# Feed-forward entry of a two-layer encoder: transposes behind the per-layer projection, products grouped by part

## The chip, the cores and the metric

The kernel runs on one core of a Trainium2 chip. The metric is device time in microseconds, the median of several runs. Before the change it is 927.31 us over three runs (926.59 to 927.93). One execution was profiled; it took 927.09 us.

## The reference, cut to what matters

Two layers work on 256 tokens of width 1024, all in float32. Each layer has a mixer of three attentions, a feed-forward part, and a gated per-layer input:

```
x = x + merged @ w_out                               # mixer
h = rms_norm(x, g_ffn)
a = depthwise_conv(h @ w_ffn_gate, conv_w, conv_b)
x = x + (gelu(a) * (h @ w_ffn_up)) @ w_ffn_down      # 1024 -> 2816 -> 1024
e = rms_norm(pe @ w_ple_proj, g_ple)                 # pe: 256 wide
g = sigmoid(rms_norm(x, g_ple_in) @ w_ple_gate)
return x + g * e
```

## The kernel before, in words

**Products in parts.** TensorE multiplies numbers of type float32r, which hold fewer bits than float32. So every operand is kept as a hi part (float32r) and a lo part (what is left), and a product is hi by hi, plus hi by lo, plus lo by hi (`mm3`).

**Weights.** The class `Stream` brings the weights in units of at most 128 x 1024 (512 KB) in a fixed order: a load on SyncE's queue into one of four `raw` buffers (L80), the hi part by ScalarE (`whi`, L91), the lo part by VectorE as `raw - whi` (`wlo`, L92), four buffers each. `get()` hands out a unit and sees to it that loads stand four units and splits two units ahead of it. `W.behind` can hang the split of a unit behind another instruction.

**Who sets the order.** A scheduler puts the instructions of each engine in order, by its own estimate of when each is ready and by priorities. `tc.high_priority(offset=HI)` lifts a stretch of code by 400. Only the first stage of layer 0 (`tc.manual_schedule`) keeps the order of the code. A change in one place can so move instructions in other places.

**PSUM.** There are four banks of 128 x 512 named `acc` (accumulators of long sums) and four named `ps` (transposes, short sums).

**Transposes.** `transpose_half` brings one half (512 columns) of a token-major tensor into column-major form: eight transposes of 128 x 128 on TensorE (L330), two banks, two column blocks k to a bank; each bank is then split by ScalarE (hi, L352) and VectorE (lo, L353), with a gain per row as the scale.

**Feed-forward entry.** After the output projection `out1` and the addition to x, ScalarE takes sums of squares (`ffnj`), GpSimd raises them to the power -1/2 (`ffnr`), VectorE makes the normed x (`xn`). TensorE does the per-layer projection `pp0`, `pp1` (24 products of 512 columns), whose results wait in the four `acc` banks, and 16 transposes `ffnT`, from which the splits make `fT`: for each of eight blocks k, hi and lo side by side, 512 columns.

**Feed-forward.** In 11 steps s, each for 256 of the 2816 hidden columns: gate `g` and up `u` with the weights stationary (128 x 128 of whi against the 512 columns of `fT`, then 128 x 128 of wlo against the 256 hi columns of `fT`), two banks i, eight k each; the convolution and GELU; then `down` of the step before, 24 products of 512 columns (`dn`). The evictions of `pp0` and `pp1` (VectorE product `e`, ScalarE square with sum `ej`, then `e0m`, a power and `reh` on GpSimd, and the scaling of `e`) are collected in `late_e` and run behind the first gate of a layer.

**Names in the start of layer 0.** `g00`, `g01` are branch gates (products of 512 columns, evicted by ScalarE with a function from a table), `uk00tok`, `uk01tok` the normed keys of the latent attention, `mk0b` and `mq0b` transposes of keys and queries, `uq1` and `dqa` projections. `sinT` and `cosT` come from `pos_col`, the positions, by a chain of small VectorE operations and one ScalarE function; GpSimd multiplies them with gains (`rpk`, `rpq`), and the rotated key `krr` goes into `uk00tok` and `uk01tok`.

Of the kernel before, what the change touches and what calls it, by code (L numbers as in the profile page):

```python
# [59 lines left out]
class Stream:  # L60


    def __init__(self, nc, pools, ahead_load, ahead_split):
        self.nc = nc
        self.raw_pool, self.hi_pool, self.lo_pool = pools
        self.al, self.asp = ahead_load, ahead_split
        self.specs = []
        self.raw = {}
        self.split = {}
        self.nl = self.ns = self.nu = 0  # L70
        self.behind = {}
# [11 lines left out]

    def _split(self):
        i = self.ns
        _, a, n = self.specs[i]
        m = a * n
        raw = self.raw.pop(i)
        hi = self.hi_pool.tile([P, 1024], F32R, tag="whi", name=f"whi{i}")
        lo = self.lo_pool.tile([P, 1024], F32R, tag="wlo", name=f"wlo{i}")  # L90
        ih = self.nc.scalar.activation(hi[:, :m], raw[:, :m], AF.Copy)  # L91
        il = self.nc.vector.tensor_tensor(lo[:, :m], raw[:, :m], hi[:, :m].bitcast(F32), op=ALU.subtract)  # L92
        for ins, b in zip((ih, il), self.behind.pop(i, (None, None))):
            if b is not None:
                self.order(ins, b)
        self.split[i] = (hi[:, :m].rearrange("p (a n) -> p a n", a=a), lo[:, :m].rearrange("p (a n) -> p a n", a=a))
        self.ns += 1
# [4 lines left out]

    def presplit(self, n):
        while self.ns < n:
            self._split()

    def get(self):
        i = self.nu
        self.nu += 1
        while self.nl < min(i + self.al + 1, len(self.specs)):  # L110
            self._load()
        while self.ns < min(i + self.asp + 1, len(self.specs)):
            self._split()
        return self.split.pop(i)
# [3 lines left out]
def kernel(ctx: ExitStack, tc: tile.TileContext, a: dict, out: bass.AP):  # L118
# [196 lines left out]

    def low(f):
# [58 lines left out]

    def transpose_half(src, h, hi, lo, gcol, name, scale=None, k_base=None):
        res = []
        for kp in range(2):  # L380
            b = bank(f"{name}T{h}{kp}")
            bv = b.rearrange("p (a n) -> p a n", a=2)
            for i in range(2):
                c = (kp * 2 + i) * P
                for t in range(NT):
                    TR(bv[:, i, t * P:(t + 1) * P], src[t][h][:, c:c + P], ident)
            k0 = (h * 4 if k_base is None else k_base) + kp * 2
            if gcol is None:
                res.append(split(hi[:, k0:k0 + 2, :], lo[:, k0:k0 + 2, :], bv, scale))
            else:  # L390
                for i in range(2):
                    res.append(split(hi[:, k0 + i, :], lo[:, k0 + i, :], bv[:, i, :], gcol(k0 + i)))
        return res

# [100 lines left out]
    def layer(l):  # L495
# [71 lines left out]
        if l == 0:  # L567
            ET = mybir.EngineType
            with tc.manual_schedule(engines={ET.Activation, ET.DVE, ET.SP, ET.PE}):
                pt = bank("gmix_ps")  # L570
                TR(pt[:, :P], mrow, ident)
                gm = const.tile([P, 8], F32, name="gmix0")
                nc.vector.tensor_copy(gm, pt[:, :8])
                W.prime(1)
                load_x(1)
                W.prime(4)
                G[0] = g = load_gains(0)
                for h in range(2):
                    transpose_half(x, h, hTh, hTl, lambda k: gm[:, k:k + 1], n_ + "mix")
                    W.presplit(1 + h)  # L580
                next(ag)
                next(ag)
                next(ag)
                mix_stats()
                load_gains2(0, g)
                for _ in ag:
                    pass
            finish_gains(0, g, last_pe[0])
        else:
            next(ag)  # L590
            next(ag)
            transpose_half(x, 1, hTh, hTl, lambda k: g["T"][:, R_MIX + k:R_MIX + k + 1], n_ + "mix")
            low(mix_stats)()
            yield from ag
# [412 lines left out]
        def T_mg(h):  # L1007
            if not mlT:
                mlT["h"] = big.tile([P, KT, S], F32R, tag="big", name=n_ + "mTh")
                mlT["l"] = big.tile([P, KT, S], F32R, tag="big", name=n_ + "mTl")  # L1010
            transpose_half(mg["m"], h, mlT["h"], mlT["l"], None, n_ + "mg", 0.5)

# [75 lines left out]
        def evict_e(h):  # L1088
            def f(accs):
                late_e.append(lambda: fin(accs))  # L1090

# [8 lines left out]
        def lhs_p(k, t):  # L1100
            return pTh[:, k, t * P:(t + 1) * P], pTl[:, k, t * P:(t + 1) * P]

        for h in range(2):
            yield from gemm(f"{n_}pp{h}", 2, 512, lhs_p, evict_e(h))
        fT = [big.tile([P, KT // 2, 2, S], F32R, tag="big", name=f"{n_}fT{h}") for h in range(2)]
        for h in range(2):
            with tc.high_priority(offset=HI):
                transpose_half(xn, h, fT[h][:, :, 0, :], fT[h][:, :, 1, :],
                               lambda k, h=h: gT[:, R_FFN + 4 * h + k:R_FFN + 4 * h + k + 1], n_ + "ffn", k_base=0)

# [33 lines left out]
        for s in range(NF // 2):  # L1144
            pb = {}
            for nm in ("g", "u"):
                bs = [bank(f"{n_}{nm}{s}{i}") for i in range(2)]
                ws = [W.get(), W.get()]
                for i in range(2):
# [11 lines left out]
                if s == 0 and nm == "g":  # L1161
                    finish_e()
# [37 lines left out]
        for h in range(2):  # L1200
            with tc.high_priority(offset=HI):
                tr = transpose_half(x, h, lTh, lTl, lambda k: gT[:, R_PIN + k:R_PIN + k + 1], n_ + "ple")
                if h == 0:
# [34 lines left out]
        if l + 1 < DEPTH:  # L1238
            gn = G[l + 1]["T"]
            transpose_half(x, 0, nh, nl, lambda k: gn[:, R_MIX + k:R_MIX + k + 1], f"L{l + 1}mix")  # L1240
        yield from p1
# [28 lines left out]
```

## Time and profile before

| what | value |
|---|---|
| median of three runs | 927.31 us (926.59 to 927.93) |
| the profiled execution | 927.09 us |
| its span in the trace | 925.3 us, so 1.8 us lie outside |
| TensorE busy | 909.6 us, 98% |
| VectorE, ScalarE, GpSimd busy | 737.6, 631.4, 82.9 us |
| moved by DMA | 155.90 MB, mean 168 GB/s |

The span is the time from the first to the last instruction in the trace, and busy time leaves out instructions that only branch, wait or start transfers. Matrix products are pipelined: the spacing of two starts says what one costs, while the length shown for one (about 0.39 us at 512 columns) holds its way through the array as well.

### The profile page before, as it was taken

To read this page: it belongs to the slowest core of one execution; us is meant where nothing else is said; L and a number is where in the kernel's file an instruction comes from. 1 tells how busy PE (TensorE), PEld (TensorE's weight loads), DVE (VectorE), ACT (ScalarE), POOL (GpSimd) and SP (SyncE) were. 2 spreads that over 40 slices of the span, in tenths; PEclk is the share of its full clock that TensorE was granted. 3 is DMA by queue.
4 is the path that set the end of the run, shared out by engine and by line. 5 is a ranking of instruction groups with operands and counts; after the bars stand their busy time and mean duration, and the time that the engine had idled before them with its cause. 6 is when DMAs were issued, how large, how long until landed. Compare 5 with 4: busy or idle time off the path is not lost.

```text
span 925.3 us, 13733 instructions
## 1 busy us (share of the span) xinstructions
PE 909.6 (98%) x4807; PEld 764.8 (83%) x4807; DVE 737.6 (80%) x1355; ACT 631.4 (68%) x1172; POOL 82.9 (9%) x149
## 2 busy tenths in 40 slices
PE   7999999999999999999999999999999999999997
PEld 6788887788788888888888888777887888888886
DVE  4899799887688778777777987989767977777784
ACT  5878876885476566665676788688655766566572
POOL 1523110010010000000112312000000100000010
PEclk9999999999999999999999999999999999999999
DMA  6755435355646666666555645343475566655642
GB/s 197 233 176 159 145 97 168 105 166 192 195 137 206 193 184 190 184 184 196 159 147 186 193 140 166 103 149 114 141 218 166 166 197 185 198 181 190 196 147 89
DMA packets 101705, 155.90 MB, mean 168 GB/s; under 512 B 7316, under 2 KB 58372, under 8 KB 101636
## 3 DMA queue, kind: packets, MB, share of 16 engines
q1 hardware_dynamic: 101636, 155.02, 54.2%
q8 instruction: 38, 0.62, 0.3%
q14 instruction: 31, 0.25, 0.1%
HBM read 153.95 MB, written 1.05 MB: 168 GB/s over the span
## 4 chain that ended last, share of the span: by engine, by line
PE 90%; DVE 4%; ACT 4%; issue 1%; DMA 1%; POOL 0%; ACTq 0%; SPq 0%; DVEq 0%; POOLq 0%
PE L1g L327 7%; PE L0g L327 7%; PE L0u L327 7%; PE L1u L327 7%; PE L0dn L327 7%; PE L1dn L327 7%; DVE wlo L92 1%; PE L0g20a L327 1%; PE L1g20a L327 1%; PE L1dva L327 1%; PE L0dva L327 1%; PE L0dka L327 1%; PE L1dka L327 1%; PE L1g00a L327 1%; PE L1g01a L327 1%; PE L0pg0a L327 1%
## 5 line engine op out<-in xcount | busy, mean ns | idle before, releaser
L92 DVE TENSOR_TENSOR wlo<-raw,whi 128x1024 fp32r<-128x1024 f32 (+3 forms) x292 | 350.6, 1206 | 86.9 <-ACT whi L91 86.2
L91 ACT ACTIVATE whi<-raw 128x1024 fp32r<-128x1024 f32 (+3 forms) x292 | 304.1, 1044 | 135.2 <-PE L0dn L327 13.1
L327 PE MATMUL L1g<-L1fT,whi 128*128 128x512 f32 x176 | 62.7, 399 | 0.0
L327 PE MATMUL L0g<-L0fT,whi 128*128 128x512 f32 x176 | 62.7, 399 | 0.0
L327 PE MATMUL L0u<-L0fT,whi 128*128 128x512 f32 x176 | 62.7, 398 | 0.0
L327 PE MATMUL L1u<-L1fT,whi 128*128 128x512 f32 x176 | 62.6, 398 | 0.0
L327 PE MATMUL L0u<-L0fT,wlo 128*128 128x256 f32 x176 | 49.4, 281 | 0.0
L327 PE MATMUL L1u<-L1fT,wlo 128*128 128x256 f32 x176 | 49.4, 281 | 0.0
L327 PE MATMUL L1g<-L1fT,wlo 128*128 128x256 f32 x176 | 49.4, 281 | 0.0
L327 PE MATMUL L0g<-L0fT,wlo 128*128 128x256 f32 x176 | 49.4, 281 | 0.0
L327 PEld LDWEIGHTS L0g<-L0fT,whi 128*128 128x128 f32 x176 | 33.1, 188 | 8.5 <-DVE L0fT L353 0.5
L327 PEld LDWEIGHTS L1g<-L1fT,whi 128*128 128x128 f32 x176 | 33.1, 188 | 8.5 <-DVE L1fT L353 0.5
L327 PEld LDWEIGHTS L1u<-L1fT,whi 128*128 128x128 f32 x176 | 33.1, 188 | 8.3
L327 PEld LDWEIGHTS L0u<-L0fT,whi 128*128 128x128 f32 x176 | 33.1, 188 | 8.3
L327 PEld LDWEIGHTS L1g<-L1fT,wlo 128*128 128x128 f32 x176 | 33.2, 189 | 0.4
L327 PEld LDWEIGHTS L0g<-L0fT,wlo 128*128 128x128 f32 x176 | 33.2, 189 | 0.4
L327 PEld LDWEIGHTS L0u<-L0fT,wlo 128*128 128x128 f32 x176 | 33.2, 189 | 0.0
L327 PEld LDWEIGHTS L1u<-L1fT,wlo 128*128 128x128 f32 x176 | 33.2, 189 | 0.0
L1171 ACT ACTIVATE L0c<-L0gs,gT 128x256 f32<-128x256 f32 x22 | 13.3, 603 | 18.5 <-DVE L0gs L1160 18.5
L1171 ACT ACTIVATE L1c<-L1gs,gT 128x256 f32<-128x256 f32 x22 | 13.3, 603 | 18.5 <-DVE L1gs L1160 18.5
L327 PE MATMUL L0dn<-whi,L0hh 128*128 128x512 f32 x88 | 24.5, 394 | 0.0
L327 PE MATMUL L1dn<-whi,L1hh 128*128 128x512 f32 x88 | 24.5, 394 | 0.0
(1736 smaller groups left out, 2483.8 us busy)
## 6 DMA issues: line engine op xcount, KB each, us to landing
raw<-in_w_in_dram SPq DMA_DIRECT2D x84, 512.0 KB
raw<-in_w_ffn_gate_dram SPq DMA_DIRECT2D x44, 512.0 KB
raw<-in_w_ffn_up_dram SPq DMA_DIRECT2D x44, 512.0 KB
raw<-in_w_ffn_down_dram SPq DMA_DIRECT2D x44, 512.0 KB
raw<-in_w_branch_dram SPq DMA_DIRECT2D x24, 512.0 KB
raw<-in_w_out_dram SPq DMA_DIRECT2D x16, 512.0 KB
raw<-in_w_ple_gate_dram SPq DMA_DIRECT2D x16, 512.0 KB
raw<-in_w_in_dram SPq DMA_DIRECT2D x8, 416.0 KB
```

Source lines behind the costliest of these rows:

```text
L91: ih = self.nc.scalar.activation(hi[:, :m], raw[:, :m], AF.Copy)
L92: il = self.nc.vector.tensor_tensor(lo[:, :m], raw[:, :m], hi[:, :m].bitcast(F32), op=ALU.subtract)
L327: last_pe[0] = nc.tensor.matmul(*args, **kw)
L1171: nc.scalar.activation(c[:, i, :], pb["g"][:, i, :], AF.Identity, scale=tap(1), bias=gT[:, R_CB + ff:R_CB + ff + 1])
```

## The change

- `transpose_half` takes both banks first and issues all eight transposes; where a gain per row is used, the blocks k alternate between the banks. The splits move into a function `finish` that is returned; most callers call it at once.
- In the feed-forward entry, the projection runs with `W.asl = 0`: the hi splits of weights still go two units ahead, the lo splits do not. The transposes of both halves are issued, then their splits at high priority; the lo splits of the next two units hang behind the last of them. The eviction of `pp0` runs at once, that of `pp1` still later.
- Gate and up: per bank, eight products with whi and then eight with wlo, where they alternated. The first gate of a layer has its banks from `acc`, does all 16 products with whi by k over both banks, then all 16 with wlo.
- `Stream` has separate functions for hi and lo splits.

```
-    def transpose_half(src, h, hi, lo, gcol, name, scale=None, k_base=None):
...
+    def transpose_half(src, h, hi, lo, gcol, name, scale=None):
+        bs = [bank(f"{name}T{h}{e}").rearrange("p (a n) -> p a n", a=2) for e in range(2)]
+        for k in range(4):
+            e, i = (k // 2, k % 2) if gcol is None else (k % 2, k // 2)
+            for t in range(NT):
+                TR(bs[e][:, i, t * P:(t + 1) * P], src[t][h][:, k * P:(k + 1) * P], ident)
+        def finish():
...
+            return [split(hi[:, k0 + k, :], lo[:, k0 + k, :], bs[k % 2][:, k // 2, :], gcol(k0 + k)) for k in range(4)]
+        return finish
...
         def evict_e(h):
             def f(accs):
-                late_e.append(lambda: fin(accs))
+                if h:
+                    late_e.append(lambda: fin(accs))
+                else:
+                    fin(accs)
...
+        W.asl = 0
         for h in range(2):
             yield from gemm(f"{n_}pp{h}", 2, 512, lhs_p, evict_e(h))
+        W.asl = 2
...
-        for h in range(2):
-            with tc.high_priority(offset=HI):
-                transpose_half(xn, h, fT[h][:, :, 0, :], fT[h][:, :, 1, :],
...
+        fins = [transpose_half(xn, h, View(fT[h], 0, 4 * h), View(fT[h], 1, 4 * h),
+                               lambda k: gT[:, R_FFN + k:R_FFN + k + 1], n_ + "ffn") for h in range(2)]
+        with tc.high_priority(offset=HI):
+            last = [f()[-1][1] for f in fins][-1]
+        for i in range(2):
+            W.behind[W.ns + i] = (None, last)
...
-                for i in range(2):
-                    c = slice(i * P, (i + 1) * P)
-                    for k in range(KT):
-                        wh, wl = ws[k // 4]
-                        xp = fT[k // 4][:, k % 4]
-                        MM(bs[i], wh[:, k % 4, c], xp.rearrange("p a n -> p (a n)"), start=k == 0, stop=False)
-                        MM(bs[i][:, :S], wl[:, k % 4, c], xp[:, 0, :], start=False, stop=k == KT - 1)
+                kinds = [(0, i, k) for i in range(2) for k in range(KT)], [(1, i, k) for i in range(2) for k in range(KT)]
+                if first:
+                    steps = sorted(kinds[0], key=lambda b: b[2]) + kinds[1]
+                else:
+                    steps = sorted(kinds[0] + kinds[1], key=lambda b: b[1])
+                for m, i, k in steps:
...
+                    if m == 0:
+                        MM(bs[i], w, xp.rearrange("p a n -> p (a n)"), start=k == 0, stop=False)
+                    else:
+                        MM(bs[i][:, :S], w, xp[:, 0, :], start=False, stop=k == KT - 1)
```

The order on TensorE in the feed-forward entry of layer 0, before: `pp1` products, the transposes `ffnT` among them, and from the rest of the projection on to the gate.

```order
L327 MATMUL L0pp1a_3057<-wlo_2994,L0pTh 128x512
L330 MATMUL L0ffnT_3079<-ident,L0xn 128x128
L330 MATMUL L0ffnT_3088<-ident,L0xn 128x128
L327 MATMUL L0pp1a_3057<-whi_2993,L0pTl 128x512
L330 MATMUL L0ffnT_3097<-ident,L0xn 128x128
L330 MATMUL L0ffnT_3106<-ident,L0xn 128x128
L327 MATMUL L0pp1a_3057<-whi_2993,L0pTh 128x512
L330 MATMUL L0ffnT_3079<-ident,L0xn 128x128 x2
L330 MATMUL L0ffnT_3097<-ident,L0xn 128x128 x2
```

The transposes stand in the middle of `pp1`. At the same place now (x2 stands for two equal rows):

```order
L345 MATMUL L0pp1a_3062<-wlo_2995,L0pTh 128x512
L345 MATMUL L0pp1a_3062<-whi_2993,L0pTl 128x512
L348 MATMUL L0ffnT_3081<-ident,L0xn 128x128 x2
L348 MATMUL L0ffnT_3082<-ident,L0xn 128x128 x2
L348 MATMUL L0ffnT_3081<-ident,L0xn 128x128 x2
L348 MATMUL L0ffnT_3082<-ident,L0xn 128x128 x2
L348 MATMUL L0ffnT_3091<-ident,L0xn 128x128 x2
L348 MATMUL L0ffnT_3092<-ident,L0xn 128x128 x2
L348 MATMUL L0ffnT_3091<-ident,L0xn 128x128 x2
L348 MATMUL L0ffnT_3092<-ident,L0xn 128x128 x2
L345 MATMUL L0g_3145<-L0fT_3079,whi_3041 128x512
```

All of `pp1` now stands ahead of the transposes, which go from bank to bank, and the gate's first product comes behind the last of them.

VectorE at the same place before, from the last `xn` on:

```order
L1082 TENSOR_SCALAR L0xn<-x_108,L0ffnr_3027 128x512
L92 TENSOR_TENSOR wlo_3148<-raw_3039,whi_3147 128x1024
L353 SCALAR_TENSOR_TENSOR L0fT_3077<-L0ffnT_3079,gT_319,L0fT_3077 128x256
L353 SCALAR_TENSOR_TENSOR L0fT_3078<-L0ffnT_3097,gT_319,L0fT_3078 128x256
L353 SCALAR_TENSOR_TENSOR L0fT_3078<-L0ffnT_3106,gT_319,L0fT_3078 128x256
```

and now:

```order
L1101 TENSOR_SCALAR L0xn<-x_108,L0ffnr_3027 128x512
L1116 TENSOR_TENSOR L0e<-L0pp0a_3038,gple_2832 128x512
L1116 TENSOR_TENSOR L0e<-L0pp1a_3061,gple_2832 128x512
L1116 TENSOR_TENSOR L0e<-L0pp1a_3062,gple_2832 128x512
L376 TENSOR_SCALAR L0e0m<-L0se_3206 128x1
L1146 TENSOR_SCALAR L0e<-L0e,L0reh_3212 128x1024
L371 SCALAR_TENSOR_TENSOR L0fT_3079<-L0ffnT_3081,gT_319,L0fT_3079 128x256
L371 SCALAR_TENSOR_TENSOR L0fT_3079<-L0ffnT_3082,gT_319,L0fT_3079 128x256
```

The products `e` of the projection and one scaling of `e` stand ahead of the first split of `fT`, where a wlo stood.

ScalarE in the start of layer 0, where `sinT` and `cosT` are made, before:

```order
L538 ACTIVATE L0araw_143<-L0Aa_221 128x416
L304 ACT_TABLE_LOAD
L304 ACTIVATE sinT<-r0.0_353 128x32
L304 ACTIVATE cosT<-r0.25_363 128x32
L243 ACT_TABLE_LOAD
L243 ACTIVATE gsc_383<-gsc_383 128x2
```

and now, some thirty instructions later in its order:

```order
L313 ACT_TABLE_LOAD
L313 ACTIVATE sinT<-r0.0_353 128x32
L90 ACTIVATE whi_695<-raw_624 128x1024
L90 ACTIVATE whi_733<-raw_660 128x512
L996 ACT_TABLE_LOAD
L996 ACTIVATE L0g_711<-L0g01a_529,L0st 128x512
L313 ACT_TABLE_LOAD
L313 ACTIVATE cosT<-r0.25_363 128x32
L996 ACT_TABLE_LOAD
L996 ACTIVATE L0g_711<-L0g01a_530,L0st 128x512
```

`sinT` and `cosT` no longer stand side by side: there are four table loads in place of two, and `cosT` stands between the evictions of the two banks of `g01`. The number of matrix products is the same in both kernels.

## Rows read from the trace of the kernel before

**Rows 1.** The page: busy time, granted clock by slice, the chain by engine.
```profile
PE 909.6 (98%) x4807; PEld 764.8 (83%) x4807; DVE 737.6 (80%) x1355; ACT 631.4 (68%) x1172; POOL 82.9 (9%) x149
...
PEclk9999999999999999999999999999999999999999
...
PE 90%; DVE 4%; ACT 4%; issue 1%; DMA 1%; POOL 0%; ACTq 0%; SPq 0%; DVEq 0%; POOLq 0%
```

**Rows 2.** TensorE's waits: for what, in total, times, longest.
```profile
PE L0ffnT L330 <- DVE L0xn L1082: 0.6, 1, 0.6
PE L0mk0b L330 <- DVE L0uk01tok L803: 0.6, 1, 0.6
```

**Rows 3.** Chain of waits from 245 us (start, length, what), and one group of the page.
```profile
263.05 5.66 PE L0u L327 x32
...
280.01 5.50 PE L0dn L327 x24
...
L327 PE MATMUL L0u<-L0fT,wlo 128*128 128x256 f32 x176 | 49.4, 281 | 0.0
```

**Rows 4.** Timeline of TensorE, 248 to 263: start, length, line, output and inputs, count, wait.
```profile
248.86 0.39 PE L327 MATMUL L0pp0a<-whi,L0pTh 128*128 128x512 f32 x1
...
251.81 0.39 PE L327 MATMUL L0pp1a<-wlo,L0pTh 128*128 128x512 f32 x1
...
253.78 1.47 PE L330 MATMUL L0ffnT<-ident,L0xn 128*128 128x128 f32 x12
...
257.14 0.50 PE L327 MATMUL L0g<-L0fT,whi 128*128 128x512 f32 x1
```

**Rows 5.** Timeline of TensorE, 111.5 to 114, uniform 256 columns.
```profile
111.78 0.28 PE L327 MATMUL L0skva<-wlo,L0hTh 128*128 128x256 f32 x1
...
113.70 0.28 PE L327 MATMUL L0skva<-whi,L0hTl 128*128 128x256 f32 x1
```

**Rows 6.** Timelines of VectorE, ScalarE and GpSimd, 243 to 270.
```profile
248.62 1.28 DVE L1057 TENSOR_TENSOR x<-x,L0out1a 128x512 f32<-128x512 f32 x2
...
252.20 1.67 DVE L1082 TENSOR_SCALAR L0xn<-x,L0ffnr 128x512 f32<-128x512 f32 x4 [0.58 <-POOL L0ffnr L374]
...
255.03 3.23 DVE L353 SCALAR_TENSOR_TENSOR L0fT<-L0ffnT,gT,L0fT 128x256 fp32r<-128x256 f32 x8
...
259.67 1.28 DVE L1094 TENSOR_TENSOR L0e<-L0pp0a,gple 128x512 f32<-128x512 f32 x2
...
263.95 0.75 DVE L1120 TENSOR_SCALAR L0e<-L0e,L0reh 128x1024 f32<-128x1024 f32 x1 [0.99 <-POOL L0reh L1119]
...
260.39 0.60 ACT L1097 ACTIVATE L0ej<-L0pp0a 128x512 f32<-128x512 f32 x1 [1.89 <-DVE L0e L1094]
...
263.04 0.55 POOL L360 TENSOR_TENSOR L0e0r<-L0e0m,mhalf 128x1 f32<-128x1 f32 x1 [0.27 <-DVE L0e0m L358]
...
266.31 1.48 POOL L360 TENSOR_TENSOR L0e1r<-L0e1m,mhalf 128x1 f32<-128x1 f32 x1 [1.56 <-DVE L0e1m L358]
```

**Rows 7.** Timeline of ScalarE, 24.7 to 54.
```profile
25.20 1.28 ACT L304 ACT_TABLE_LOAD   x1
...
45.42 0.63 ACT L91 ACTIVATE whi<-raw 128x512 fp32r<-128x512 f32 x1 [0.87 <-PE L0g01a L327]
...
48.51 0.69 ACT L977 ACTIVATE L0g<-L0g01a,L0st 128x512 f32<-128x512 f32 x1 [0.56 <-PE L0g01a L327]
```

**Rows 8.** Timelines of TensorE, VectorE and GpSimd, 26 to 54.
```profile
45.23 0.27 PE L330 MATMUL L0mk0b<-ident,L0uk00tok 128*96 128x128 f32 x1
...
46.12 0.31 PE L330 MATMUL L0mk0b<-ident,L0uk01tok 128*96 128x128 f32 x1 [0.62 <-DVE L0uk01tok L803]
...
46.84 0.47 PE L327 MATMUL L0g01a<-whi,L0hTh 128*128 128x512 f32 x1
...
47.05 0.56 DVE L773 TENSOR_TENSOR L0uq01tok<-L0uq0a,L0uq01ri 128x384 f32<-128x384 f32 x1 [0.52 <-POOL L0uq01ri L739]
...
27.44 0.25 POOL L257 TENSOR_TENSOR rpq<-cosT,gbc 128x32 f32<-128x32 f32 x1
```

More of the change, by code (lines that the diff above doesn't have):

```diff
@@ L69, in __init__ @@
         self.split = {}
[L70 removed]
+        self.his = {}
+        self.nl = self.nh = self.ns = self.nu = 0
         self.behind = {}
@@ L82, in _load, with split_hi, split_lo @@
         self.nl += 1
-    def _split(self):
+    def split_hi(self):
+        i = self.nh
+        _, a, n = self.specs[i]
+        m = a * n
+        hi = self.hi_pool.tile([P, 1024], F32R, tag="whi", name=f"whi{i}")[:, :m]
+        ih = self.nc.scalar.activation(hi, self.raw[i][:, :m], AF.Copy)
+        if self.behind.get(i, (None, None))[0] is not None:
+            self.order(ih, self.behind[i][0])
+        self.his[i] = hi
+        self.nh += 1
+    def split_lo(self):
         i = self.ns
@@ L87, in _split @@
         m = a * n
[L88 to L96, printed above, removed]
+        hi = self.his.pop(i)
+        lo = self.lo_pool.tile([P, 1024], F32R, tag="wlo", name=f"wlo{i}")[:, :m]
+        il = self.nc.vector.tensor_tensor(lo, self.raw.pop(i)[:, :m], hi.bitcast(F32), op=ALU.subtract)
+        if self.behind.get(i, (None, None))[1] is not None:
+            self.order(il, self.behind[i][1])
+        self.split[i] = (hi.rearrange("p (a n) -> p a n", a=a), lo.rearrange("p (a n) -> p a n", a=a))
         self.ns += 1
@@ L111, in get @@
             self._load()
-        while self.ns < min(i + self.asp + 1, len(self.specs)):
-            self._split()
+        hi, lo = (min(i + n + 1, len(self.specs)) for n in (self.asp, self.asl))
+        while self.nh < hi or self.ns < lo:
+            if self.nh < hi:
+                self.split_hi()
+            if self.ns < lo:
+                self.split_lo()
         return self.split.pop(i)
@@ L314, in positions_setup, with __init__, __getitem__ @@
                                 compare_op=ALU.is_ge, fill=NEG)
+    class View:
+        def __init__(self, t, i, k0):
+            self.t, self.i, self.k0 = t, i, k0
+        def __getitem__(self, key):
+            return self.t[:, key[1] - self.k0, self.i, :]
     def low(f):
@@ L376, in x_stats @@
         return res
-    def transpose_half(src, h, hi, lo, gcol, name, scale=None, k_base=None):
[L379 to L382, printed above, removed]
-            for i in range(2):
[L384 to L387, printed above, removed]
-            if gcol is None:
[L389 to L393, printed above, removed]
+    def transpose_half(src, h, hi, lo, gcol, name, scale=None):
[5 more added lines that the diff above has]
+        def finish():
+            k0 = h * 4
+            if gcol is None:
+                return [split(hi[:, k:k + 2, :], lo[:, k:k + 2, :], b, scale) for k, b in zip((k0, k0 + 2), bs)]
+            return [split(hi[:, k0 + k, :], lo[:, k0 + k, :], bs[k % 2][:, k // 2, :], gcol(k0 + k)) for k in range(4)]
+        return finish
     def gemm(name, nk, n, lhs, evict, alloc=None):
@@ L1160, in layer @@
                     nc.vector.tensor_tensor(o, bs[i][:, :S], o, op=ALU.add)
-                if s == 0 and nm == "g":
+                if first:
                     finish_e()
```

25 lines of the change are left out of this document (12 added, 13 removed).

## The prediction

> **What bounds the kernel now.** I read the page first. TensorE is busy 98% of the span, and the chain that ended last is 90% TensorE [rows 1]. So the time is a count of matrix products times their spacing, plus the few places where TensorE waits. The granted clock stands at the upper level, 2.4 GHz, in every slice [rows 1]; the clock is no term of what follows. The list of TensorE's waits comes next: behind the start-up, whose waits are for transfers, no wait is above 0.6 us, and two of those 0.6 us waits lie where the change works, the feed-forward entry (ffnT waits for xn) and mk0b in the mixer of layer 0 (for uk01tok) [rows 2]. So 0.6 us per layer is all that can be had there from waiting alone, and the larger handle is the spacing of the products. For that the chain of waits gives whole blocks, and the timeline single starts.
>
> **Spacing in the feed-forward.** A block of 32 products (16 pairs, one of 512 columns with whi and one of 256 with wlo) takes 5.66 us [rows 3], which is 5.66/16 = 354 ns a pair. There are four groups of 176 such pairs, 704 in all: one group stands in [rows 3], the others are gate and up of either layer. What a pair costs when nothing alternates is read elsewhere: uniform 512-column products start at 248.86 and, 13 products later, at 251.81, which is 227 ns each [rows 4]; the 24 products of dn, also 512 wide, take 5.50 us, 229 ns each [rows 3]; uniform 256-column products start at 111.78 and, 16 later, at 113.70, 120 ns each [rows 5]. So 227 + 120 = 347 ns uniform against 354 alternating, or 349 by the dn block. The alternation costs 5 to 7 ns a pair. After the change eight products of 512 come before eight of 256, which leaves one alternation in eight pairs: the gain is 7/8 of 5 to 7 ns, times 704, or 3.1 to 4.3 us. I take 3.7, the middle, since dn reads other operands and pp0 and pp1 are nearer in time. Bounds: 4.3 at best; at worst nothing, if the 7 ns come from the sum of two widths and not from their order.
>
> The Trainium skill, page "TensorE: Matmul & The Clock Gate", section "Back-to-back issue gap", gives a spacing at full clock that depends on the columns of each product alone (N/2.4 plus 2.5 ns), so by it the order earns nothing and this term is 0. The trace does not agree with its size: it would make the pair 325 ns where 354 is measured.
>
> **The feed-forward entry.** Before, from the start of pp0 at 248.86 to the first gate product at 257.14 pass 8.28 us [rows 4]. The work in it is 24 projection products of 227 ns (5.45) and 16 transposes (12 of them take 1.47 us, so 1.96), 7.4 us. The rest, 0.9 us, is the wait of 0.6 for xn [rows 2] and that for fT ahead of the gate. Now all 24 projection products come ahead of the 16 transposes, so xn is long ready, and TensorE ends the transposes at 248.86 + 7.4 = 256.2. If the gate could start there, a layer would gain 0.9 us. But the evictions of pp0 and pp1 and the scaling of e, which before came behind the gate's start, now stand on VectorE and ScalarE ahead of the fT splits. On ScalarE, from 249.3, where the first half of the x addition ends (two take 1.28 from 248.62 [rows 6]), stand five squares with sum (0.6 each [rows 6]) and three whi (about 1.0), so fT's first hi half ends near 255.7. On VectorE the four e products (two take 1.28 [rows 6]) and xn (four take 1.67 [rows 6]) end at 255.2, as the last of them needs the end of pp1 at 254.3. Then come e0m, the power on GpSimd, and the e scaling of 0.75 [rows 6], and only behind it the first lo half of fT (eight take 3.23, so 0.4 each [rows 6]). The GpSimd power took 0.55 for one token block and 1.48 for the other [rows 6]. With 0.55 it is 255.2 + 0.15 + 0.55 + 0.22 + 0.75 + 0.4 = 257.3, with 1.48 it is 258.2. The gate's first product therefore starts at 257.4 to 258.3 where it started at 257.14: the wait removed in front of xn returns in front of fT. I take +0.3 us a layer (the short power, which is what the first scaling of before had), +0.6 for both layers; bounds per layer are -0.9 (the scaling hides) and +1.2.
>
> Behind that, the four held-back lo splits run after the last fT split. From the gate's start VectorE needs 7 x 0.4 for fT, 0.75 for the second e scaling, 0.15, and 1.2 for the first wlo, 4.9 us; TensorE has 16 hi products of the gate and 7 of up ahead of the first lo product, 23 x 0.227 = 5.2 us. The lo splits that follow are 1.2 us apart; the products between them take about as long. I cost them at nothing; the cover is those 23 hi products, and without it each of the splits costs up to 1.2 us.
>
> **The start of layer 0.** Nothing in the words of the change speaks of it, but the order moves there. The transposes of the mixer's entry alternate banks, so that ScalarE and VectorE no longer take turns on one bank there. The list of TensorE's waits names no wait for those splits [rows 2], and the products behind them wait for weights in any case, so I cost it at 0. What costs is further on: the load of pos_col goes from behind the fifth block of weights to behind the eleventh, so the sine and cosine chain comes some 15 us later, and sinT and cosT, before computed together between two table loads of 1.28 us [rows 7], now have four loads, two of them between the halves of a gate eviction. The last of these go like this: ScalarE ends whi16 at 46.05 (45.42 + 0.63 [rows 7]), a load until 47.3, the eviction of the first bank of g01 (0.69 [rows 7]) until 48.0, a load until 49.3, cosT until 49.5. Then GpSimd makes the four cosine products (0.25 each [rows 8]), 50.5, and VectorE some eight small ones with uq01tok (0.56 [rows 8]) among them, which I put at 1.5 us together, until 52.0; uk01tok is the last. TensorE did mk0b at 46.12 [rows 8]; now it has first the last 12 of g01 and six dqa: it gains 46.84 - 45.23 = 1.6 us [rows 8] on g01 by not having been at mk0b, ends it 12 x 0.227 behind 45.23, at 48.0, and six dqa of 0.23 take it to 49.4. It waits there until 52.0, 2.6 us, in place of 0.6: +2.0 us. I take +1.8, since VectorE's work is then partly ahead. Bounds: 0 (if the chain is early enough to be hidden, as before it was), and 3.2, one more load of 1.28 in series.
>
> The Trainium skill, page "ScalarE: Activation LUTs", section "Rules for kernel authors", says to group functions by table set and to do all of one set before another; its section "What ACT_TABLE_LOAD costs" puts a switch at about 2.66 us with a drain. This speaks against the change. Here the load shows as 1.28 us [rows 7], so the measured figure decides; by the page's figure an estimate of the wait at mk0b would grow by 2 x 1.36 = 2.7 us, and the sum would be 928.6.
>
> **Sum.** The profiled execution before took 927.09 us (span 925.3, 1.8 outside), 0.22 under the median of 927.31. 927.09 - 3.7 + 0.6 + 1.8 = 925.8; on the scale of the median 926.0. I predict 925.9. A measurement of this kernel can tell about 0.2% (1.85 us) from no change; 925.9 lies 0.4 us inside.
>
> **Rivals.**
> A. The sum as it stands, 925.9, own range 923.8 to 928.0. Chance 0.50. The bound of 925.46 lies 0.4 below the forecast, so a little over a third of it is faster: 0.20 faster, 0.30 same.
> B. The waits vanish: the scaling of e does not hold fT up (-0.9 a layer), and the cosine comes in time (0). 927.3 - 3.7 - 1.8 = 921.8. For it: VectorE has idle stretches before 255 in which the e products fit. Against: the scaling waits for pp1's end whatever else happens. Chance 0.17, all faster.
> C. The order of hi and lo is worth nothing, and the rest is as summed: 927.3 + 2.4 = 929.7, or 928.5 with the stall at mk0b halved. For it: no row here shows grouped products of one weight pair. Against: the rows of 227 and 120. Chance 0.18: half same, half slower (0.09 each).
> D. Slower: the held-back lo splits become the bound at the feed-forward entry. The place is the first gate product of 256 columns, which waits for wlo on VectorE behind the second e scaling. If the GpSimd power takes 1.48 both times, the gate starts 1.0 later and each of the four splits is late by one split, 1.2: 2.2 us a layer more, 925.9 + 4.4 = 930.3. It decides from 0.3 us of lateness (5.2 against 4.9). For it: the power of 1.48 us stands in the trace. Against: the first of before took 0.55. Chance 0.11, all slower.
> E. The table loads cost more than their 1.28 us: 928.6, from the bound of 3.2 and up. Chance 0.04, same.
> Together: faster 0.37, same 0.43, slower 0.20. The range leaves out half of B and half of D and reaches from 921.8 to 930.0.
>
> **What would show each step.** Grouping: gate and up blocks of 32 products from the third on take 5.57 us or less, with 512-column starts 227 to 229 ns apart and 256-column starts 120; if they take 5.66, C holds. Entry: the first gate product starts 8.5 us after pp0, with TensorE waiting about 1 us for fT's lo half; if it starts 7.4 after, B, and if TensorE waits for a wlo within the next 8 us, D. Start: TensorE's list of waits has mk0b with 2 to 3 us where it had 0.6, and ScalarE shows four table loads from 40 to 50; if it has no such wait, my walk of the cosine is wrong. If the wait there is over 4 us, or the granted clock falls behind it, the forecast is too low.

## The result and the profile after

The changed kernel takes 934.02 us (median of six runs, 933.26 to 934.39); the kernel before, beside it, 927.62 us (926.59 to 929.05). The ratio is 1.0067, 95% interval 1.0054 to 1.008: 6.4 us slower, outside the predicted range and on the other side of no change. The profiled execution took 934.39 us, 7.3 more than the 927.09 of before.

The page shows that TensorE does the same 4807 products in the same busy time as in [rows 1], and that the chain that ended last has lost 9 points of TensorE, four of them to VectorE:

```profile
PE 909.5 (98%) x4807; PEld 766.7 (82%) x4807; DVE 736.7 (79%) x1355; ACT 634.3 (68%) x1174; POOL 85.0 (9%) x149
...
PE 81%; DVE 8%; ACT 5%; issue 2%; DMA 2%; POOL 2%; SPq 0%; ACTq 0%; DVEq 0%; POOLq 0%
```

So the loss stands in waits, and the equal busy time is itself a sum: quicker blocks in the feed-forward and slower products elsewhere, both shown below. The list of TensorE's waits (for what, total, times, longest) shows where it waits; [rows 2] had 0.6 and 0.6:

```profile
PE L0mk0b L348 <- DVE L0uk00tok L822: 2.4, 1, 2.4
...
PE L0g L345 <- DVE L0fT L371: 1.5, 1, 1.5
PE L1g L345 <- DVE L1fT L371: 1.5, 1, 1.5
PE L0g L345 <- ACT whi L90: 1.1, 1, 1.1
PE L0g00a L345 <- DVE wlo L102: 1.1, 2, 0.7
PE L0dqb L348 <- DVE L0tok L650: 1.1, 1, 1.1
PE L1g L345 <- ACT whi L90: 0.6, 1, 0.6
...
PE L0dqa L345 <- DVE wlo L102: 0.4, 1, 0.4
```

A list of waits says nothing of products that run slower. For that I set the start of the same product in two traces side by side. This table gives the start in the kernel named less the start in the kernel before, in us, each from the timeline of TensorE of one profiled execution (the start-up, with its waits for x and for the first weights, moves these from execution to execution: e1_blocks and e4_nohold have the same order of products on TensorE up to pp0 and stand 1.6 apart there). What counts is the difference between neighbouring columns.

| kernel | m0s (layer 0) | pp0 L0 | gate L0 | first dn L0 | pleT L0 | pp0 L1 | gate L1 | first dn L1 | pleT L1 |
|---|---|---|---|---|---|---|---|---|---|
| after | 4.31 | 6.14 | 6.76 | 8.80 | 7.02 | 7.08 | 7.68 | 8.98 | 7.24 |
| e1_blocks | 1.91 | 1.87 | 2.48 | 3.68 | 1.90 | 1.87 | 2.46 | 3.77 | 2.04 |
| e2_banks | 3.12 | 4.87 | 4.87 | 4.87 | 4.87 | 4.80 | 4.80 | 4.80 | 4.78 |
| e3_group | 0.25 | 0.24 | 0.24 | -0.02 | -1.68 | -1.68 | -1.69 | -1.93 | -3.55 |
| e4_nohold | 0.35 | 0.31 | 1.03 | 1.09 | -0.57 | -0.45 | 0.27 | 1.94 | 0.32 |
| e9_entry | 0.72 | 0.66 | 1.28 | 6.20 | 6.18 | 6.15 | 6.75 | 12.52 | 12.53 |
| e10_entry_nohold | 1.91 | 1.87 | 2.58 | 2.22 | 2.18 | 2.18 | 2.90 | 2.55 | 2.55 |

(m0s are the scores of the latent attention, pleT the transposes behind the feed-forward part, the first dn stands at the end of step 1.) Read for the changed kernel, from left to right: 6.1 us are lost before the feed-forward part of layer 0 begins; the entry costs 0.6 in each layer; the first two steps cost 2.0 and 1.3; the steps behind them give back 1.8 and 1.7.

**The start of layer 0.** The timeline of TensorE (start, length, line, output and inputs, count, wait), where [rows 8] had a wait of 0.62:

```profile
49.93 0.39 PE L345 MATMUL L0dqa<-whi,L0hTl 128*128 128x512 f32 x1
52.69 0.29 PE L348 MATMUL L0mk0b<-ident,L0uk00tok 128*96 128x128 f32 x1 [2.37 <-DVE L0uk00tok L822]
...
54.56 0.63 PE L345 MATMUL L0dqa<-wlo,L0hTh 128*128 128x512 f32 x1
54.99 0.63 PE L345 MATMUL L0dqa<-whi,L0hTl 128*128 128x512 f32 x1
```

The wait is 2.37 us. Behind it the products of 512 columns show a length of 0.63 where they had 0.39 ahead of it, and start 0.43 apart, not 0.23. The windows of the same stretch (length, busy time and count of TensorE, weight loads, VectorE, ScalarE and GpSimd, granted clock, DMA share, GB/s) say why:

```profile
50.00:53.00 3.00, 0.64 (x5) 0.33 (x4) 2.38 (x15) 2.93 (x4) 1.03 (x5) 1.00 0.98 323
53.00:54.00 1.00, 1.00 (x10) 0.83 (x8) 1.00 (x7) 0.64 (x2) 0.00 (x0) 0.76 0.20 75
54.00:57.00 3.00, 3.00 (x10) 2.28 (x9) 2.53 (x4) 0.64 (x3) 0.00 (x0) 0.51 0.27 42
57.00:60.00 3.00, 3.00 (x20) 2.75 (x18) 1.93 (x3) 2.81 (x5) 0.00 (x0) 1.00 0.38 139
```

TensorE had been busy 0.64 of 3 us; then the granted clock is at 0.51, the lower level of 1.2 GHz, for some 3 us, with TensorE busy all the time. Six dqa products that take 6 x 0.23 at full clock took 6 x 0.43: 1.2 us, and the transposes around them some tenths. By busy time alone the stretch looks full, 3.00 of 3.00, and the page, whose slices are 23 us long, shows a 9 for the clock in every slice.

**What released mk0b.** The chain of waits, and the timelines of ScalarE and VectorE, at cosT:

```profile
47.86 1.85 POOL L0uq01ri L758
49.71 0.25 POOL rpq L267
```

```profile
48.28 1.28 ACT L313 ACT_TABLE_LOAD   x1
49.78 0.23 ACT L313 ACTIVATE cosT<-r0.25_363 128x32 f32<-128x32 f32 x1 [0.22 <-DVE r0.25_363 L312]
...
47.62 1.82 DVE L102 TENSOR_TENSOR wlo<-raw,whi 128x1024 fp32r<-128x1024 f32 x2
...
49.57 0.18 DVE L312 TENSOR_SCALAR r0.25_363<-r0.25_363 128x32 f32<-128x32 f32 x1
```

The four table loads are there, each 1.28 as in [rows 7]; the one ahead of cosT ends at 49.56, yet cosT waits 0.22 longer for VectorE, and the chain runs over GpSimd, whose products with the gains (`rpq`, `rpk`) start at 49.71 because a power (`L0uq01ri`, 1.85 us) stands ahead of them. VectorE stands close behind: it makes the last steps of cosT's operand only after two lo splits of weights (1.82 us from 47.62). So the loads did not decide, but by little: the three engines end within 0.2 us of one another.

**The entry.** The chain of waits ahead of the first gate of layer 0:

```profile
261.33 0.20 POOL L0se L1142
...
261.79 0.56 POOL L0e0r L378
...
262.70 0.75 DVE L0e L1146
263.45 0.40 DVE L0fT L371
...
263.90 1.76 PE L0g L345 x6
```

pp0 starts at 255.00 in this trace, so the gate comes 8.90 behind it, where [rows 4] had 8.28. It is the chain of the prediction: power, scaling of e, first lo part of fT. Ahead of the power it runs over ScalarE's squares (`ej`), with a whi of 0.82 among them, and not over VectorE's products; the last square ends 6.26 behind pp0's start, where the prediction had the last product at 6.34 (255.2 less 248.86).

**The first steps.** SyncE's queue in the timeline (start, length, line), and the chain of waits ahead of the second gate of layer 1:

```profile
249.44 3.09 SPq L81 DMA_DIRECT2D raw<-in_w_ffn_up_dram  x2
269.16 1.17 SPq L81 DMA_DIRECT2D raw<-in_w_ffn_gate_dram  x2
```

```profile
722.60 2.37 DVE wlo L102 x2
...
725.02 5.86 DMA raw<-in_w_ffn_gate_dram
...
730.90 1.07 ACT whi L90
...
732.02 4.93 PE L1g L345 x28
```

A lo split is the last reader of its `raw` buffer. With the lo splits held back behind fT, all four buffers stay taken, and SyncE issues no weight load from 252.5 to 269.2. The transfer of the next unit therefore starts late, the hi split behind it too, and TensorE waits 1.1 (layer 0) and 0.6 (layer 1) for a whi, not for a wlo. The chain shown is that of layer 1. In layer 0 it is longer: ScalarE idles 2.08 us for a late load of `down` weights before their hi split, and the whi that TensorE then waits for stands behind an operation of the convolution (`L0c`, 286.52) that itself waited 0.89 for VectorE. That this too goes back to the held-back lo splits rests on e4_nohold below, where both waits are gone.

**The blocks.** The chain of waits in the third step, to be set against [rows 3] (5.66 and 5.50):

```profile
310.77 5.56 PE L0g L345 x32
316.33 5.59 PE L0u L345 x32
321.92 5.47 PE L0dn L345 x24
```

### The profile page after: what moved, and what is told of

The parts are those of the page before. It is cut to its first block, busy times and chain, and to the rows that moved or that the text cites. A ratio compares the mean times of both kernels' runs of the same rounds, so it can differ in the third digit from the quotient of the medians.

```text
span 932.5 us, 13715 instructions
## 1 busy us (share of the span) xinstructions
PE 909.5 (98%) x4807; PEld 766.7 (82%) x4807; DVE 736.7 (79%) x1355; ACT 634.3 (68%) x1174; POOL 85.0 (9%) x149
## 4 chain that ended last, share of the span: by engine, by line
PE 81%; DVE 8%; ACT 5%; issue 2%; DMA 2%; POOL 2%; SPq 0%; ACTq 0%; DVEq 0%; POOLq 0%
PE L0g L345 7%; PE L0u L345 6%; PE L0dn L345 6%; PE L1dn L345 6%; PE L1u L345 6%; PE L1g L345 6%; DVE wlo L102 3%; PE L0g20a L345 1%; PE L1g20a L345 1%; PE L1dva L345 1%; PE L1g00a L345 1%; PE L1dka L345 1%; PE L1g01a L345 1%; PE L0pg0a L345 1%; PE L1sqa L345 1%
## 5 line engine op out<-in xcount | busy, mean ns | idle before, releaser
L345 PE MATMUL L0g<-L0fT,whi 128*128 128x512 f32 x176 | 44.6, 393 | 2.8 <-DVE L0fT L371 1.5
L345 PE MATMUL L1g<-L1fT,whi 128*128 128x512 f32 x176 | 44.6, 393 | 2.1 <-DVE L1fT L371 1.5
L345 PE MATMUL L0u<-L0fT,whi 128*128 128x512 f32 x176 | 44.6, 392 | 0.0
L345 PE MATMUL L1u<-L1fT,whi 128*128 128x512 f32 x176 | 44.6, 392 | 0.0
L345 PEld LDWEIGHTS L0g<-L0fT,whi 128*128 128x128 f32 x176 | 32.1, 188 | 9.9 <-DVE L0fT L371 2.1
L345 PEld LDWEIGHTS L1g<-L1fT,whi 128*128 128x128 f32 x176 | 32.1, 188 | 9.1 <-DVE L1fT L371 2.0
L345 PEld LDWEIGHTS L0u<-L0fT,whi 128*128 128x128 f32 x176 | 31.6, 189 | 5.6
L345 PEld LDWEIGHTS L1u<-L1fT,whi 128*128 128x128 f32 x176 | 31.7, 189 | 5.6
L345 PEld LDWEIGHTS L1u<-L1fT,wlo 128*128 128x128 f32 x176 | 24.1, 190 | 1.7
L345 PEld LDWEIGHTS L0u<-L0fT,wlo 128*128 128x128 f32 x176 | 24.1, 190 | 1.7
L345 PEld LDWEIGHTS L1g<-L1fT,wlo 128*128 128x128 f32 x176 | 24.0, 190 | 1.7
L345 PEld LDWEIGHTS L0g<-L0fT,wlo 128*128 128x128 f32 x176 | 24.0, 190 | 1.7
L345 PE MATMUL L0u<-L0fT,wlo 128*128 128x256 f32 x176 | 24.7, 282 | 0.0
L345 PE MATMUL L1u<-L1fT,wlo 128*128 128x256 f32 x176 | 24.7, 282 | 0.0
L345 PE MATMUL L1g<-L1fT,wlo 128*128 128x256 f32 x176 | 24.5, 282 | 0.0
L345 PE MATMUL L0g<-L0fT,wlo 128*128 128x256 f32 x176 | 24.5, 282 | 0.0
```

The costliest lines, as they stand in the source:

```text
L345: last_pe[0] = nc.tensor.matmul(*args, **kw)
```

## The experiments

The times of before that stand beside a run are those of the same chip.

### Where the six microseconds of layer 0 come from

The first two kernels take the bank alternation of the mixer's entry in layer 0 out of the change (e1_blocks), and put it alone into the kernel before (e2_banks). The edit of e1_blocks against the changed kernel, with `alt=False` passed by the call in the first stage of layer 0 only:

```
-            e, i = (k // 2, k % 2) if gcol is None else (k % 2, k // 2)
+            e, i = (k % 2, k // 2) if alt and gcol is not None else (k // 2, k % 2)
...
```

> The changed kernel, but the transposes of layer 0's mixer entry go block by block into the banks as before; all else of the change stays. This alone gives the start of layer 0 its old order on every engine. Theory S (the start costs 6.1 of the 6.4 us): 928.6 us, since in the changed kernel TensorE is 6.1 us late at the first feed-forward and another 1.0 us over the two feed-forwards. Theory F (the feed-forward entries are what costs, and delays of the start are made up later): 932 or more.

Measured: 928.27 us (926.86 to 929.15, 11 runs) against 927.87, ratio 1.0 (0.9991 to 1.0009). Theory S (928.6) holds. The wait at mk0b is 0.6 again. The table has +1.9 at pp0 of layer 0, which is start-up of this execution: 0.9 of it stands there at the first product of g00, and g00 waits 1.1 for a wlo.

e2_banks against the kernel before, called in the mixer's entry of layer 0:

```
+    def transpose_alt(src, h, hi, lo, gcol, name):
+        bs = [bank(f"{name}T{h}{e}").rearrange("p (a n) -> p a n", a=2) for e in range(2)]
+        for k in range(4):
+            for t in range(NT):
+                TR(bs[k % 2][:, k // 2, t * P:(t + 1) * P], src[t][h][:, k * P:(k + 1) * P], ident)
...
-                    transpose_half(x, h, hTh, hTl, lambda k: gm[:, k:k + 1], n_ + "mix")
+                    transpose_alt(x, h, hTh, hTl, lambda k: gm[:, k:k + 1], n_ + "mix")
```

> The kernel before with one edit: in layer 0's mixer entry the transposes go alternately to two banks, as in the change. Theory S: 933.7 us (927.6 + 6.1), with a wait of 2.4 us at mk0b and six products of dqa at 427 ns behind it. Theory F: 927.6 to 929.

Measured: 933.04 us (931.93 to 933.83, 5 runs) against 927.87, ratio 1.0056 (1.0043 to 1.0068). Theory S (933.7) holds. So this one detail, which nobody would call the subject of the change, carries some 5 of its 6.4 us, through the order that the scheduler makes of the rest; why the scheduler answers in this way is not shown. Its profiled execution, the shortest of the five at 931.93, has the wait but not the slow products. The windows, in the columns of above:

```profile
50.00:53.00 3.00, 0.65 (x4) 0.24 (x2) 2.14 (x13) 2.94 (x4) 1.27 (x6) 1.00 0.96 298
...
54.00:57.00 3.00, 3.00 (x20) 2.55 (x20) 2.88 (x6) 2.05 (x4) 0.00 (x0) 1.00 0.22 25
```

The same wait of 2.35 us, TensorE as little busy as above, the same order, and the granted clock stays at 1.00, with 20 products in the last three microseconds where there were 10. From the first product of mk0b to m0s, the same 76 products in the same order, pass 15.12 us here and 16.56 in the changed kernel: 1.4 us for the lower clock. (The lateness at m0s, 3.12 and 4.31, shows only 1.2 of it, because the wait ended 0.24 earlier in the changed kernel.) A fall behind the wait happens in some executions and not in others.

Two more kernels were to price it apart. e7_fill0 moves one group of g01 products ahead of mk0b in the order of the code; e8_fill18 adds 18 products whose results are overwritten, so that TensorE is not idle there.

```
-g00 g00 cT g00 g00 g01 ukv0 uq0 g01 g01 Tmk0 g01 Tmq0 uq1 dq ...
+g00 g00 cT g00 g00 g01 ukv0 uq0 g01 g01 g01 Tmk0 Tmq0 uq1 dq ...
```

```
+                if name == "L0mk0" and pr == 0:
+                    prev = last_pe[0]
+                    for _ in range(18):
+                        MM(b.rearrange("p a n -> p (a n)"), hTh[:, 0, 0:P], hTh[:, 0:2, :].rearrange("p a n -> p (a n)"), start=True, stop=True)
+                        order(last_pe[0], prev)
```

> Control of e8: the changed kernel with the transposes mk0b named one place later in the written order of the mixer (behind the last g01). Both theories: within 0.7 us of the changed kernel, 933.4 to 934.7, with the wait of 2.4 us at mk0b, and in most executions six products of 427 ns behind it.

> As e7_fill0, with 18 more products of 512 columns (hTh by hTh, into the bank that the first transposes of mk0b overwrite) between the last g01 and mk0b, 4.1 us of work that nothing uses, in the time in which TensorE otherwise has six dqa (1.4 us) and waits; those six come behind mk0b. Theory C (behind the wait the granted clock falls to 1.2 GHz for some 3 us, which costs 1.6 to 1.9 us on top of the wait): the clock stays at 2.4 GHz, dqa are 227 ns apart, and the time is that of e7 or 0.3 us less, although 4.1 us of work were added and 1.4 us moved behind the wait. Rival W (the wait alone costs): 1.4 us above e7.

Measured: 932.84 us (four runs: 930.3, 932.59, 933.09, 934.64) for e7_fill0 and 934.11 us (933.86 to 934.28, four runs) for e8_fill18, against 927.99. The timeline of TensorE in e8_fill18:

```profile
48.41 4.24 PE L345 MATMUL L0mk0b<-L0hTh 128*128 128x512 f32 x18
52.83 0.32 PE L348 MATMUL L0mk0b<-ident,L0uk00tok 128*96 128x128 f32 x1 [0.18 <-DVE L0uk00tok L827]
```

With the filler the clock is at 1.00 in all windows from 45 to 60, and the four runs lie within 0.4 us, where those of e7_fill0 lie 4.3 apart. That the filler keeps the clock up is not shown by this: the mean granted clock is 0.999 or 1.0 in three of the four runs of e7_fill0 too (930.3, 932.59, 933.09) and 0.997 only in the slowest, and those three alone lie 2.8 apart. e7_fill0 itself came out 0.6 below its range. e8_fill18 came out 1.3 above e7_fill0, nearly the number of rival W (1.4), but not for W's reason: the wait at mk0b shrank to 0.18, while six dqa products that had run ahead of it moved behind it and another wait came (1.2 us, mq0b for uq01tok). So the sum of the two is no gain, and the price of the clock can't be read from these two times.

### The grouping alone

e3_group is the kernel before with eight products of 512 columns ahead of eight of 256, per bank, in all steps:

```
-                    for k in range(KT):
-                        wh, wl = ws[k // 4]
+                    for m, k in [(m, k) for m in range(2) for k in range(KT)]:
+                        w = ws[k // 4][m][:, k % 4, c]
...
```

> The kernel before with one edit: gate and up do eight products with whi and then eight with wlo for each bank, in every step. Theory G (a change of width costs about 6 ns a pair): blocks of 32 products take 5.57 instead of 5.66 us, 44 blocks, 923.6 us. Rival (the spacing is by width alone, or what is won is lost to waits for the splits): 927.6.

Measured: 924.51 us (923.54 to 924.66, 5 runs) against 927.87, ratio 0.9962 (0.9949 to 0.9974): 3.4 us faster. Theory G (923.6) is 0.9 too low, the rival (927.6) 3.1 too high. It is the best version of this study and beats both kernels. Its blocks, in the chain of waits:

```profile
302.07 5.56 PE L0g L327 x32
307.63 5.59 PE L0u L327 x32
313.22 5.47 PE L0dn L327 x24
```

### The entry and the held-back lo splits

e4_nohold is e1_blocks without the three edits that hold lo splits back:

```
-        W.asl = 0
...
-        W.asl = 2
...
-        for i in range(2):
-            W.behind[W.ns + i] = (None, last)
```

> As e1_blocks, but the lo splits of weights are not held back at the feed-forward entry. Theory R (held-back lo splits keep their raw buffers, so the next loads start late and the gate of the second step waits for whi): that wait, 1.1 us in layer 0 and 0.6 in layer 1, is gone, against e1_blocks -1.7 us, 926.9. Rival (holding them back saves more at the gate's start, where two splits of 1.2 us then stand ahead of fT): 929 to 931.

Measured: 926.86 us (925.39 to 928.0, 11 runs), ratio 0.9988 (0.998 to 0.9997). Theory R (926.9) holds. No wait for a whi is left, SyncE issues weight loads at 249.04, 256.54 and 265.87, and the first two steps of layer 0 cost 0.06 (gate to first dn in the table) where they cost 1.2 in e1_blocks. Layer 1 costs 1.7 there with no new wait. The windows of TensorE (busy time, granted clock, DMA share, GB/s) around the gate of layer 0 and that of layer 1, behind the same wait of 1.6 us for fT:

```profile
256.00:258.00 2.00, 0.52 (x5) 1.00 0.16 24
258.00:260.00 2.00, 1.77 (x7) 1.00 0.85 279
260.00:262.00 2.00, 2.00 (x10) 1.00 0.65 222
```

```profile
710.00:712.00 2.00, 0.44 (x2) 1.00 0.40 104
712.00:714.00 2.00, 1.92 (x7) 0.75 0.89 265
714.00:716.00 2.00, 2.00 (x6) 0.50 0.44 155
```

One execution, the same wait twice: once the clock stays, once it falls to the lower level and costs 1.6 us. In layer 0, holding lo splits back thus costs 1.1 us; in layer 1 the fall hides it, and the medians differ by 1.4 us for both layers together (928.27 and 926.86). The wait for fT costs its length and, by chance, as much again. Against e3_group (924.51), which has the grouping alone, e4_nohold is still 2.3 us slower: the new entry does not pay even without the holding back.

e5_late is e1_blocks with the eviction of pp0 late too, as before the change; e6_late_nohold is that without the holding back.

```
-                if h:
-                    late_e.append(lambda: fin(accs))
-                else:
-                    fin(accs)
+                late_e.append(lambda: fin(accs))
```

> As e1_blocks (928.3), but both evictions of the per-layer projection are late, behind the first gate, as before the change. Theory E (the products and the scaling of e, with the power on GpSimd between, hold up fT: 1.5 us of TensorE waiting a layer): the first product on fT starts 6.5 to 7.5 us after pp0 starts, not 8.9, and the wait for fT falls to 0.3 or less. What is won there is worth 1 to 1.4 us a layer only if the held-back lo splits then come early as well; I expect 925.5 to 926.5. Rival (the lo splits and their loads set the first step, not fT): 928.3, with the wait moved to wlo or whi.

> As e4_nohold (926.9), but both evictions of the projection are late: what is left of the change is the grouping, the transposes behind the projection and the alternate banks there. Theory: two lo splits of 1.2 us stand ahead of fT and e no longer does, the first product on fT starts 7.5 to 8 us after pp0 (8.3 before the change, 9.0 in e4_nohold); 924.0, level with e3_group. Rival (a transposes' order of its own is worth nothing): 924.5 to 925.5.

Measured: 929.8 us (928.75 to 930.29, 11 runs), ratio 1.0019 (1.001 to 1.0028), for e5_late, and 928.56 (926.83 to 929.03, 11 runs), ratio 1.0003 (0.9994 to 1.0012), for e6_late_nohold. Both theories of e6_late_nohold, and mine of e5_late, miss: taking the scaling of e out of the way doesn't free the gate. The two runs do not single out the scaling, for the first gate still takes its banks from `acc`, where the late pp0 and pp1 now lie until they are evicted (in e6_late_nohold a weight load of the gate waits for pp0's bank). The scheduler puts up's products first, and these wait for fT (1.5 us in e5_late, 2.3 in e6_late_nohold in each layer) behind a whi or a wlo that stands ahead of fT's splits. The first product on fT starts 8.9 and 9.6 us after pp0, not earlier than in e1_blocks. The rival of e5_late had the place, waits for a wlo of 1.1 and 0.8, but lies 1.5 us too low. Behind the 2.3 us the clock falls in layer 0 of e6_late_nohold (first two windows) and stays in layer 1 (third):

```profile
258.00:260.00 2.00, 1.40 (x4) 1.14 (x5) 2.00 (x6) 1.14 (x3) 0.00 (x0) 0.72 0.78 246
260.00:262.00 2.00, 2.00 (x7) 1.52 (x6) 2.00 (x5) 0.69 (x2) 0.00 (x0) 0.50 0.06 22
...
714.00:716.00 2.00, 1.92 (x8) 1.61 (x9) 2.00 (x6) 0.78 (x3) 0.00 (x0) 1.00 0.73 232
```

### The entry without the grouping

The last two kernels are e1_blocks (e9_entry) and e4_nohold (e10_entry_nohold) with hi and lo products alternating again in all steps, the first gate too:

```
-                    steps = sorted(kinds[0], key=lambda b: b[2]) + kinds[1]
+                    steps = sorted(kinds[0] + kinds[1], key=lambda b: (b[1], b[2]))
...
-                    steps = sorted(kinds[0] + kinds[1], key=lambda b: b[1])
+                    steps = sorted(kinds[0] + kinds[1], key=lambda b: (b[1], b[2]))
```

> The entry alone: layer-0 mixer entry block by block as in e1_blocks, gate and up with hi and lo products alternating as before the change, in the first gate too. Sum theory: entry and grouping add up, so e1_blocks (928.27) less the grouping of e3_group (-3.4) gives 931.7, before 927.9. Rival: with alternating products the second product of the first gate needs a lo part at once, so that the held-back lo splits stand in the way of the first gate; then each layer waits some 2 us more for wlo than in e1_blocks, 935 to 936, and the grouping of the first gate is part of the entry and can't be told from it.

> As e9_entry, without holding lo splits back. Sum theory: e4_nohold (926.86) less the grouping (-3.4) gives 930.3. Rival: the alternating first gate meets weights that are ready only where lo splits run ahead, so this is the same as e9_entry within 1 us.

Measured: 939.98 us (939.61 to 941.32, 4 runs) against 927.81, ratio 1.0133 (1.0116 to 1.015), for e9_entry; 928.59 (927.83 to 930.12, 10 runs), ratio 1.001 (1.0 to 1.0019), for e10_entry_nohold. The waits of TensorE in e9_entry:

```profile
PE L1g L345 <- DVE wlo L102: 2.5, 1, 2.5
PE L0g L345 <- DVE wlo L102: 2.2, 1, 2.2
```

The rival holds, and at more than its price: with alternating products the held-back lo splits stand in the way at once. From the waits on, the granted clock is at 0.50, from 260 to 266 in layer 0 and again from 722 to 726 in layer 1, which is part of the price. The two first steps cost 4.9 and 5.8 us (table). The grouped first gate is what makes the holding back bearable, so the two are one design.

e10_entry_nohold came out 1.7 below the sum, and its rival (the same as e9_entry) fell by 11 us. Part of the 1.7 can be seen in its blocks in the chain of waits, here the second and third step:

```profile
271.14 5.55 PE L0g L345 x32
276.68 5.55 PE L0u L345 x32
...
287.70 5.64 PE L0g L345 x32
293.34 5.65 PE L0u L345 x32
```

All four blocks alternate. The first two run at 5.55/16 = 347 ns a pair, as if nothing alternated; then, from the step behind the first dn on, it is 353 to the end. In the kernel before the slower pace stands already in the first up block [rows 3]. Three quick blocks a layer make 0.6 us for both layers; the other 1.1 is open.

## Why the prediction was wrong, step by step

**The start of layer 0 (+1.8, bounds 0 to 3.2; measured +6.1).** This step failed, and with it the forecast. The order and the length of the wait at mk0b were read rightly: 2.4 us against 2.6 put down. In part that is luck, for the chain that was added up, over the table loads, was not the last one: a power on GpSimd and two lo splits on VectorE ended within 0.2 us of it. What failed is the sentence that the clock is no term of what follows. The prediction's last part says that the forecast is too low if the granted clock falls behind the wait, and it fell: 1.4 us (16.56 against 15.12 from mk0b to m0s). The second fault is to end the walk at mk0b. The pieces that the list of waits names are 2.4 - 0.6 at mk0b, 0.4 at dqa for a wlo, and 1.1 at dqb for its token, which is late because the stages ahead of it moved: 3.3 with no clock in it, 4.7 with it. Of the remaining 1.4, 0.2 is start-up (TensorE reaches g00 0.8 earlier and waits 1.1 there for a wlo). 1.2 lies in dqa, dka and dva, where more products of 512 columns than before follow one another at 0.31 to 0.40 us and not at 0.23; e2_banks has the same 1.2 (its 48 dqa products take 11.48 us with waits taken off, against 10.92 before). What holds up these products is not shown.

That these microseconds belong to the bank alternation in one place, and not to the feed-forward entry, is shown by e1_blocks and e2_banks. Rival E, the table loads, fell: 1.28 us each, and cosT waited for VectorE behind one. The Trainium skill, page "ScalarE: Activation LUTs", section "What ACT_TABLE_LOAD costs", puts a switch at about 2.66 us, of which about 1.28 are the load and the rest a drain. The load agrees. The drain does not show: the load from 46.28 ends at 47.56, and the eviction behind it starts at 47.58. (By the page's figure the prediction's extra is 2 x 1.38, not 2 x 1.36; its 928.6 hardly moves.)

**The entry (+0.3 a layer, bounds -0.9 to +1.2; measured +0.6).** Mechanism right, size half of what came. 8.90 us from pp0 to the gate against the 8.5 written down, with the short power (0.56) as taken. What the walk had left out is the addition `L0se` on GpSimd, 0.20, and the handovers between engines, 0.02 to 0.08 each.

**The held-back lo splits (0; measured +1.1 to +2.0 a layer).** The arithmetic on VectorE held: no product of the feed-forward waits for a wlo in the changed kernel. The step that failed is the cover named for them, which looked at the products that a late lo part delays and not at the buffer that it keeps. The lo split is the last reader of `raw`, so the weight queue stood still for 17 us and the hi part of the next unit came late. e4_nohold takes the holding back away, and the wait for whi goes with it: gate to first dn is 0.06 in layer 0, against 1.2. Rival D named the right cause, the held-back lo splits, and a price near it, 2.2 a layer, but another place and another wait: the first gate's 256-column products, for a wlo. That wait comes where the first gate alternates (e9_entry, 2.2 and 2.5 us), and with the short power of 0.55 us, where D had made the long one its condition. Of the 2.0 in the changed kernel's layer 0, 0.5 is one product of the next gate that now stands ahead of dn and waits for its whi there; the next gate has one product less to do.

**The grouping (-3.7; measured -3.4).** Right in size: e3_group gives -3.4, and blocks of 5.56 and 5.59 are what was asked for (5.57). Rival C fell. But the reason was not quite right. I had taken 5 to 7 ns as the price of changing the width. e10_entry_nohold runs 96 alternating products (48 pairs) at 347 ns a pair, and then the same at 353. So alternating by itself has no price; it can run at either of two paces, and the grouped order stays near the quicker one. What sets the pace isn't settled: the products, their operands and their order are the same in the two stretches. The Trainium skill, page "TensorE: Matmul & The Clock Gate", section "Back-to-back issue gap", gives the formula of the columns alone, which the prediction used, for a single product, and says that in a stream of weight loads and products both set the spacing. By the formula a pair is 325 ns, an estimate. No run here is at that: the pairs take 347 to 354, and the same columns at two paces.

**The sum.** By lateness in the profiled executions: 6.1 at the start, 1.2 for two entries, 3.3 for the first steps, -3.5 for the others, 7.1 us, against 7.3 between the two profiled executions and 6.4 between the medians. The terms of the forecast made -1.3. Of the 8.4 between them, 4.3 is the start of layer 0 and 3.3 the lo splits.

## What to carry to other kernels

When a scheduler orders the program, price the whole order and not the edit: follow a moved chain past the first wait that it makes, since the stages behind it move too. A wait on TensorE like those here (1.6 to 2.4 us) is to be priced at its length and, with some chance, 1.4 to 1.6 us more in products at the lower clock behind it. Before an instruction is held back, ask which buffer it is the last to read and who waits for that buffer.

## What the runs showed of the hardware that was not expected

- The granted clock falls to 1.2 GHz behind some short waits and not behind others of the same length: it fell behind 2.37 us (after) and did not behind 2.35 (e2_banks, e7_fill0); behind 2.28 us it fell in layer 0 and stayed in layer 1 of one execution (e6_late_nohold), behind 1.65 us it stayed in layer 0 and fell in layer 1 (e4_nohold). It then holds for some 3 us of full work and costs 1.4 to 1.6 us. What decides is not shown. It splits the times of one kernel: the three runs of e6_late_nohold with a mean granted clock of 0.999 took 926.83 to 927.95 us, the eight with 0.997 took 928.14 to 929.03, 1.3 us more in the mean.
- The same alternating stream of products of 512 and 256 columns runs at 347 or at 353 ns a pair, and changes from one to the other at a dn block (e10_entry_nohold, in both layers). What decides is not shown.
